# Making the low part of every fourth weight tile with a second ScalarE pass and an adding transfer instead of a VectorE subtraction

## The chip, the cores and the metric

One core of a Trainium2 chip runs one decoder layer on 256 tokens. The metric is the device time of one execution in microseconds (us). The engines are TensorE (PE: matmuls; PEld: its weight loads), VectorE (DVE), ScalarE (ACT), GpSimd (POOL) and SyncE (SP, which here only issues transfers). Sixteen DMA engines move the data.

## The reference

One layer on x of shape (1, 256, 1024), in float32. Cut to what matters:

```
h    = rms_norm(x, ln1_g)
q, k, v, z, xbc, dt, gate_a, gate_b = split(h @ w_in)           # w_in: 1024 x 10272
y_a  = moba_attention(norm(q), norm(k), v) @ w_o_attn
y_b  = mamba2_mixer(z, xbc, dt, ...) @ w_o_ssm
x    = x + (sigmoid(gate_a) * y_a + sigmoid(gate_b) * y_b) @ w_out
x    = x + (silu(h2 @ w_gate) * (h2 @ w_up)) @ w_down           # h2 = rms_norm(x, ln2_g)
x    = x + (p @ w_ple_proj) * sigmoid(h3 @ w_ple_gate)          # h3 = rms_norm(x, ln3_g)
```

Nearly all the work is matrix products of 256 token rows with some 100 MB of float32 weights, each of which is read from memory once.

## The kernel before

**Three products for one.** A float32 operand is cut into two parts of a faster matmul type (fp32r): a high part, which is the operand rounded, and a low part, which is the operand less the high part. A product is then a_high·w_high + a_high·w_low + a_low·w_high, three matmuls into one accumulator (`Panel.step`; `rows_step` for the panels that are computed with the weights as the stationary operand).

**Weight tiles.** The weights come in tiles of 128 partitions x 2 x 512 values, 512 KB each (`w_tiles`). A tile has three buffers: `raw`, as it is loaded (four buffers in turn), `wh`, the high part (four), and `wl`, the low part (five). For each tile, `load_tiles` issues the load on SP (L346) and calls `split_w`, where ScalarE writes wh from raw (the helper `act`, L213) and VectorE writes wl = raw - wh (L334). TensorE reads wh first and wl straight after it, 12 to 24 matmuls to a tile. A buffer is written again when its last reader is done: wh of tile n+4 when TensorE is done with tile n, wl of tile n+5 likewise, raw of tile n+4 when the split of tile n is done. The first eight tiles go another way (`load_first`); from there on every tile goes through `load_tiles`, and this document counts tiles from there, from 0 to 179.

**What sets the order.** TensorE's products over the weights follow one another in the order of the table `PANELS` (and after it w_o_attn, w_out, the gate and up weights, w_down, w_ple_gate); each is pinned behind the one before it (`queue`, `follow`). Between them stand background products: the transposes and convolution inputs, the attention scores and values, and the state-space scan. Generators (`Filler`) hand these out by due times that are written out by hand (`LAG`). All other engines get their order from the framework's scheduler: it goes through a timeline of its own and takes what is ready there by priority. The weight split has the first rank ("w"), then the emptying of accumulators ("ev"), then the background ("bg"). So a change to one helper can move instructions on every engine. Each engine runs its instructions strictly in the order that it was given, and one that waits holds up all that stand behind it.

**GpSimd's part.** It has few instructions between 50 and 310 us: 16 mask-like selections for the scan (`decay_rows`, L726, written to the four buffers `rr`, each of which must first be released by TensorE), eight inverse square roots of eight columns for the q and k norms (L662), and the four pairs that make `r_ssm` for the group norm (L462, L463).

Of the kernel before, what the change touches and what calls it, by code (L numbers as in the profile page):

```python
# [13 lines left out]
ALU = mybir.AluOpType  # L14
# [43 lines left out]
    ('yb', 3, None),  # L58
]
NFF = 11  # L60

NORMED = 5
BY_ROWS = [kind in ('xbc', 'z') and n >= NORMED for n, (kind, _, _) in enumerate(PANELS)]
# [91 lines left out]
def tile_layer(ctx: ExitStack, tc: tile.TileContext, head, xk, pt, vec, w_dt, w_big, w_dn2, w_pp, out):  # L155
    nc = tc.nc
# [3 lines left out]
    @contextmanager  # L160
    def prio(c):
        saved = tc.cur_priority
        tc.cur_priority = counters[c]
        yield
        counters[c] = tc.cur_priority
        tc.cur_priority = saved
# [45 lines left out]
    def act(o, i, f=AF.Copy, **kw):  # L212
        return nc.scalar.activation(o, i, f, **kw)  # L213
# [12 lines left out]
    def follow(ins, before):  # L226
        tc.add_manual_dep(
            ins, before.name, mybir.DependencyInfo(mybir.DependencyClass.NoSync, mybir.DependencyReason.DATA),
            reason="order of the tensor engine")
# [85 lines left out]
        load_head(xraw[k // 2][:, k % 2 : k % 2 + n])  # L315

    chunk_no = [0]

    def w_tiles():
        return (sb.tile([P, 2, 512], F32, tag="raw", bufs=4, name=nm("raw")),  # L320
                sb.tile([P, 2, 512], F32R, tag="wh", bufs=4, name=nm("wh")),
                sb.tile([P, 2, 512], F32R, tag="wl", bufs=5, name=nm("wl")))

    def split_w(tiles, js=slice(0, 2), c=WHOLE, on=None):

        raw, wh, wl = (t[:, js, c] for t in tiles)
        if on is None:
            rounded = act(wh, raw)
        elif on == c:
            rounded = nc.vector.tensor_copy(wh, raw)  # L330
        else:
            rounded = act(tiles[1][:, js, HALVES[0]], tiles[0][:, js, HALVES[0]])
            nc.vector.tensor_copy(tiles[1][:, js, on], tiles[0][:, js, on])
        nc.vector.tensor_sub(wl, raw, wh.bitcast(F32))  # L334
        return rounded
# [4 lines left out]
    def load_tiles(src, nk, behind=None):  # L340


        with prio("w"):
            for k in range(0, nk, 2):
                tiles = w_tiles()
                nc.sync.dma_start(tiles[0], src[:, k : k + 2])  # L346
                rounded = split_w(tiles)
                if behind is not None and behind[k // 2] is not None:
                    follow(rounded.ins, behind[k // 2])
                yield tiles  # L350

    def load(src, nk):

        return [part for tiles in load_tiles(src, nk) for part in parts_of(tiles)]
# [40 lines left out]
    def next_src():  # L395
        c = w_big[chunk_no[0]]
        chunk_no[0] += 1
        return c
# [657 lines left out]
    for n, (kind, i, _) in enumerate(PANELS):  # L1056
# [5 lines left out]
        if BY_ROWS[n]:  # L1062
            to = s4([4, T])
            for jj in range(2):
                tiles = load_tiles(next_src(), 4)
                wide = (kind, i) in WIDE
                if wide:
                    u = s2([2, T])
                else:
                    ps = psg.tile([P, 2, T], F32, tag="g", name=nm("g"))  # L1070
                for j, w in enumerate(tiles):
                    if wide:
                        ps = psg.tile([P, 512], F32, tag="g", name=nm("g"))
                    for k in range(8):
                        rows_step(ps if wide else ps[:, j], w, k, h_n, wide)
                    if wide:
                        with prio("ev"):
                            act(u[:, j], ps[:, T:])
                            nc.vector.tensor_add(u[:, j], ps[:, :T], u[:, j])  # L1079
                evac_rows(kind, i, jj, u if wide else ps, to)  # L1080
            fill.spawn(end_rows(kind, i, to), 0)
            continue
# [165 lines left out]
    h2 = res2.acts[0] + res2.acts[1]  # L1248
    for n in range(2 * NFF):

        tiles = load_tiles(next_src(), 4, [(None, res2.scaled), (fill.rounded, fill.rounded)][n] if n < 2 else None)
        pss = [psg.tile([P, 512], F32, tag="g", name=nm("g")) for _ in range(2)]
        if n == 0:

            tiles = list(tiles)
            for k in range(8):
                for ps, w in zip(pss, tiles):
                    rows_step(ps, w, k, h2, True)
        else:
            for ps, w in zip(pss, tiles):  # L1260
                for k in range(8):
                    rows_step(ps, w, k, h2, True)
        gate_up(n, *pss)
# [24 lines left out]
def _layout(i):  # L1288
# [5 lines left out]
    def kt(w):  # L1294

        return w.reshape(-1, P, w.shape[1]).transpose(1, 0, 2)

    def chunks(w, c0, k0, nk):
        return kt(w[k0 * P : (k0 + nk) * P, c0 : c0 + 512])
# [20 lines left out]

    gu = kt(gu).reshape(P, 8, 2, 2 * NFF, P).transpose(3, 0, 2, 1, 4).reshape(2 * NFF, P, 4, 512)
    big += [chunks(f["w_out"], 512 * n, 4 * g, 4) for g in range(2) for n in range(2)]
# [39 lines left out]
```

## Time and profile before

| | |
|---|---|
| time, median of 3 runs | 587.11 us (586.98 to 587.22) |
| span of the profiled execution, first to last instruction | 586.0 us |
| around the span (median less span) | 1.1 us |
| PE / DVE / ACT / POOL busy | 580.7 / 454.3 / 347.8 / 48.8 us |
| L334, wl = raw - wh, on VectorE | 193 instructions, 230.8 us |
| L213, wh from raw, on ScalarE | 192 instructions, 199.4 us |
| moved by DMA | 104.98 MB |

The page gives no time of the profiled execution but its span; the median of the runs stands for it. Busy time is the time in which an engine executes, without its waits. In a group's row stand the line, the engine, the operation, what it writes and reads by the program's names, the count, then busy time in us and the mean of one in ns, then the idle time of the engine just ahead of these instructions, with what ended most of it. In a row of the timeline stand the start in us, the duration in us, and in brackets the idle time ahead of it with what released it. A line number can be that of a helper: every ScalarE activation has L213 and nearly every matmul L232.

### The profile page before, as it was taken

Reading aid. Unit: us, or ns where it says so; the run is one execution under the profiler, and the core shown is the slowest. Engines: PE = TensorE matmul, PEld = TensorE weight load, DVE = VectorE, ACT = ScalarE, POOL = GpSimd, SP = SyncE. Lnnn points to the kernel's source line nnn. Section 1 sums busy time; section 2 is a strip of 40 time slices with the busy share of each in tenths; the row PEclk is TensorE's granted clock in tenths of the full one; section 3 lists DMA queues with packets and bytes.
Section 4 is the critical chain, followed back from the end, with each engine's and each line's share of the span. In section 5 each row is a group of like instructions: output and inputs, shape, how many; then the busy total and the mean of one; then the engine's idle time right before and its main releaser. Section 6 shows DMA issues by size and latency. Waiting matters only on the chain.

```text
span 586.0 us, 8990 instructions
## 1 busy us (share of the span) xinstructions
PE 580.7 (99%) x3245; PEld 493.6 (84%) x3245; DVE 454.3 (78%) x763; ACT 347.8 (59%) x598; POOL 48.8 (8%) x62
## 2 busy tenths in 40 slices
PE   9999999999999999999999999999999999999996
PEld 8887888988988888888887888888888888888885
DVE  6668899998889999998856765787777777546464
ACT  7846675775757569566654345775555555435452
POOL 2021120000412502000000000000000000000010
PEclk9999999999999999999999999999999999999999
DMA  9875545454553653554554675375556555665531
GB/s 325 312 233 181 180 152 181 144 181 148 160 161 102 204 186 112 193 150 141 155 186 145 200 261 175 105 248 190 184 185 189 188 192 181 192 196 188 181 107 72
DMA packets 33419, 104.98 MB, mean 179 GB/s; under 512 B 3712, under 2 KB 7136, under 8 KB 33376
## 3 DMA queue, kind: packets, MB, share of 16 engines
q1 hardware_dynamic: 33088, 104.03, 55.1%
q8 instruction: 25, 0.41, 0.3%
q10 hardware_dynamic: 288, 0.39, 0.2%
q14 instruction: 18, 0.15, 0.1%
HBM read 103.28 MB, written 1.06 MB: 178 GB/s over the span
## 4 chain that ended last, share of the span: by engine, by line
PE 99%; DVE 0%; ACT 0%; issue 0%
PE g L232 89%; PE pb L232 6%; PE pb L254 3%; PE pb L266 1%; ACT s L213 0%; DVE s L1281 0%; DVE s L1282 0%
## 5 line engine op out<-in xcount | busy, mean ns | idle before, releaser
L334 DVE TENSOR_TENSOR wl<-raw,wh 128x1024 fp32r<-128x1024 f32 (+2 forms) x193 | 230.8, 1199 | 102.4 <-ACT wh L213 101.7
L213 ACT ACTIVATE wh<-raw 128x1024 fp32r<-128x1024 f32 (+2 forms) x192 | 199.4, 1041 | 176.7 <-PE g L232 94.5
L232 PE MATMUL g<-wh,s 128*128 128x512 f32 (+1 forms) x836 | 262.3, 391 | 0.0
L232 PE MATMUL g<-s,wh 128*128 128x512 f32 (+1 forms) x736 | 236.1, 380 | 0.0
L232 PEld LDWEIGHTS g<-wh,s 128*128 128x128 f32 x836 | 156.9, 189 | 32.0 <-issue 0.5
L232 PE MATMUL g<-s,wl 128*128 128x256 f32 x672 | 177.2, 281 | 0.0
L232 PE MATMUL g<-wl,s 128*128 128x512 f32 (+1 forms) x418 | 161.1, 388 | 0.0
L232 PEld LDWEIGHTS g<-s,wh 128*128 128x128 f32 x736 | 129.9, 189 | 21.0 <-DVE s L1111 0.2
L232 PEld LDWEIGHTS g<-s,wl 128*128 128x128 f32 x672 | 127.0, 189 | 7.1
L232 PEld LDWEIGHTS g<-wl,s 128*128 128x128 f32 x418 | 78.5, 188 | 15.7 <-DVE wl L334 0.4
L213 ACT ACTIVATE s<-s 128x256 fp32r<-128x256 f32 (+4 forms) x75 | 41.4, 555 | 13.7 <-DVE s L1166 5.0
L213 ACT ACTIVATE s<-g 128x256 f32<-128x256 f32 (+1 forms) x94 | 38.4, 411 | 5.9 <-PE g L232 3.3
L213 ACT ACTIVATE s<-pb 128x512 f32<-128x512 f32 (+3 forms) x53 | 24.5, 484 | 15.7 <-PE pb L254 7.9
L596 DVE SCALAR_TENSOR_TENSOR s<-s,vecs,s 128x255 f32<-128x255 f32 (+2 forms) x72 | 33.6, 489 | 0.0
L232 PE MATMUL pb<-s,s 128*64 128x128 f32 (+5 forms) x336 | 29.3, 294 | 0.0
L232 PEld LDWEIGHTS pb<-s,s 128*64 128x64 f32 (+2 forms) x336 | 24.0, 158 | 6.2 <-issue 3.2
L726 POOL TENSOR_SCALAR_AFFINE_SELECT rr<-a_h 128x512 fp32r<-128x512 f32 x16 | 17.0, 1079 | 121.5 <-PE pb L232 104.7
L254 PE MATMUL pb<-ident,s 128*128 128x128 f32 x170 | 25.7, 273 | 0.0
L254 PEld LDWEIGHTS pb<-ident,s 128*128 128x128 f32 x170 | 20.5, 140 | 3.8 <-issue 0.3
L1175 POOL TENSOR_TENSOR tiny<-ss 128x1 f32<-128x1 f32 x4 | 1.4, 340 | 266.8 <-ACT s L213 266.8
L213 ACT ACTIVATE s<-s,vecs 128x256 f32<-128x256 f32 (+1 forms) x40 | 20.3, 557 | 3.2 <-DVE s L1079 3.1
L662 POOL TENSOR_TENSOR tiny<-tiny,mhalf 128x8 f32<-128x8 f32 x8 | 15.3, 1913 | 42.2 <-DVE tiny L660 38.3
(138 smaller groups left out, 328.6 us busy)
## 6 DMA issues: line engine op xcount, KB each, us to landing
raw<-in_w_big SPq DMA_DIRECT2D x176, 512.0 KB
raw<-in_head SPq DMA_DIRECT2D x4, 512.0 KB
s<-in_xk SPq DMA_DIRECT2D x4, 512.0 KB
raw<-in_head SPq DMA_DIRECT2D x6, 256.0 KB
s<-e_d SPq DMA_DIRECT2D x8, 128.0 KB
raw<-in_w_pp SPq DMA_DIRECT2D x2, 512.0 KB
raw<-in_w_dn SPq DMA_DIRECT2D x2, 512.0 KB
out<-s SPq DMA_DIRECT2D x3, 256.0 KB
```

Source lines behind the costliest of these rows:

```text
L213: return nc.scalar.activation(o, i, f, **kw)
L232: ins = nc.tensor.matmul(o, lhsT, rhs, start=start, stop=stop).ins
L254: queue(nc.tensor.transpose(o, i, ident[: i.shape[0], : i.shape[0]]).ins, main)
L266: nc.tensor.matmul(pw[:, :P], zero, zero, start=True, stop=True)
L334: nc.vector.tensor_sub(wl, raw, wh.bitcast(F32))
L596: stt(cc[j][:, sft:], pu[:, j, : T - sft], cw[j][3 - sft], cc[j][:, sft:], op0=ALU.mult, op1=ALU.add)
L662: nc.gpsimd.tensor_tensor(f, ms, mhalf, op=ALU.pow)
L726: nc.gpsimd.affine_select(r, bcast(a_h[:, c, h0 : h0 + 4].bitcast(F32), P), pattern=[[0, 4], [1, P]], compare_op=ALU.is_ge, fill=0.0, base ...
L1175: nc.gpsimd.tensor_add(sss, self.ss[:, tt, 0:1], self.ss[:, tt, 1:2])
```

## The change

For 18 of the tiles, numbers 16, 20, 24 and so on to 84, VectorE's subtraction is left out. ScalarE makes a second pass over raw and writes the rounded tile with the sign turned into wl, and GpSimd then issues a transfer that reads the same 512 KB of the weights from memory once more and adds them to wl. The other tiles are made as before.

```diff
+BY_DMA = range(16, 88, 4)
...
+    tile_no = [-1]
...
                 tiles = w_tiles()
                 nc.sync.dma_start(tiles[0], src[:, k : k + 2])
-                rounded = split_w(tiles)
+                tile_no[0] += 1
+                if tile_no[0] in BY_DMA:
+                    rounded = act(tiles[1], tiles[0])
+                    act(tiles[2], tiles[0], scale=-1.0)
+                    nc.gpsimd.dma_start(tiles[2], src[:, k : k + 2], accum_op=ALU.add)
+                else:
+                    rounded = split_w(tiles)
```

The scheduler then gives every engine a somewhat other order. In what follows, line numbers are nine higher after the change, and the numbers in the names of buffers are not the same in both.

On ScalarE, around tile 64: its buffers are wh_2758 before, and wl_2771 and wh_2770 after. The rows with `s_486` are the exponentials of one step of the attention, `g_2534` and `g_2545` are an accumulator that is being emptied. Before:

```order
L213 ACTIVATE wh_2729<-raw_2728 128x1024
L213 ACTIVATE s_473_2497<-g_2534 128x256
L213 ACTIVATE s_503_2632<-pb_2630 128x512
L213 ACTIVATE s_486_2539,tiny_2538<-s_486_2539,tiny_2537 128x128
L213 ACTIVATE s_486_2539,tiny_2538<-s_486_2539,tiny_2537 128x256
L213 ACTIVATE s_486_2539,tiny_2538<-s_486_2539,tiny_2537 128x128
L213 ACTIVATE wh_2758<-raw_2757 128x1024
L213 ACTIVATE s_486_2539,tiny_2538<-s_486_2539,tiny_2537 128x256
```

and after:

```order
L215 ACTIVATE s_452_2402<-s_473_2508,vecs 128x256
L215 ACTIVATE s_503_2644<-pb_2642 128x512
L215 ACTIVATE s_486_2550,tiny_2549<-s_486_2550,tiny_2548 128x128
L215 ACTIVATE s_486_2550,tiny_2549<-s_486_2550,tiny_2548 128x256
L215 ACTIVATE s_486_2550,tiny_2549<-s_486_2550,tiny_2548 128x128
L215 ACTIVATE s_486_2550,tiny_2549<-s_486_2550,tiny_2548 128x256
L215 ACTIVATE wl_2771<-raw_2769 128x1024
L215 ACTIVATE wh_2770<-raw_2769 128x1024
```

The new pass stands ahead of the tile's own wh, and both behind the last of the exponentials. So it is, with a few other rows between at some tiles, at all 18 tiles: wl ahead of wh.

On GpSimd, at the same place. Before:

```order
L726 AFFINE_SELECT rr_2958<-a_h 128x512
L726 AFFINE_SELECT rr_2962<-a_h 128x512
L462 TENSOR_SCALAR tiny_2646<-tiny_2641 128x2
L463 TENSOR_TENSOR r_ssm<-tiny_2646,mhalf 128x2
L462 TENSOR_SCALAR tiny_3030<-tiny_3025 128x2
```

and after:

```order
L735 AFFINE_SELECT rr_2971<-a_h 128x512
L735 AFFINE_SELECT rr_2975<-a_h 128x512
L354 DMA wl_2771<-in_w_big 128x1024
L471 TENSOR_SCALAR tiny_2658<-tiny_2653 128x2
L472 TENSOR_TENSOR r_ssm<-tiny_2658,mhalf 128x2
L354 DMA wl_2993<-in_w_big 128x1024
L354 DMA wl_3102<-in_w_big 128x1024
L354 DMA wl_3221<-in_w_big 128x1024
```

The 18 new transfers stand between the selections, the norms' inverse roots and the r_ssm pairs: whatever waits there holds up a transfer behind it, and a transfer that waits for ScalarE holds them up.

On TensorE, at one step of the attention scores (rows that write `pb`) in the products of tiles 20 and 21 (`g_1026` before, `g_971` and `g_1028` after). Before:

```order
L232 MATMUL g_1026<-s_77_452,wl_1022 128x256
L232 MATMUL pb_987<-s_65_429,s_100_560 128x128
L232 MATMUL pb_986<-s_65_429,s_100_560 128x128
L232 MATMUL g_1026<-s_79_458,wh_1021 128x512
L232 MATMUL g_1026<-s_79_458,wl_1022 128x256
```

and after:

```order
L234 MATMUL g_971<-s_81_464,wl_966 128x256
L234 MATMUL pb_989<-s_65_429,s_100_560 128x128
L234 MATMUL pb_988<-s_65_429,s_100_560 128x128
L234 MATMUL g_971<-s_81_464,wh_965 128x512
L234 MATMUL g_971<-s_81_464,wl_966 128x256
```

The first two score products have moved ahead by some ten rows, into the tile before. The weight products keep their order; background products move among them. Runs of background products that stand between weight products number 74 before and 79 after, with the same products in them.

## The prediction

> **What bounds the kernel now.** I read the page first: the engines' shares, the chain that ended last, and the groups that the change touches.
>
> ```profile
> span 586.0 us, 8990 instructions
> PE 580.7 (99%) x3245; PEld 493.6 (84%) x3245; DVE 454.3 (78%) x763; ACT 347.8 (59%) x598; POOL 48.8 (8%) x62
> ...
> PE 99%; DVE 0%; ACT 0%; issue 0%
> ...
> L334 DVE TENSOR_TENSOR wl<-raw,wh 128x1024 fp32r<-128x1024 f32 (+2 forms) x193 | 230.8, 1199 | 102.4 <-ACT wh L213 101.7
> L213 ACT ACTIVATE wh<-raw 128x1024 fp32r<-128x1024 f32 (+2 forms) x192 | 199.4, 1041 | 176.7 <-PE g L232 94.5
> ```
>
> The chain that ended last is TensorE for 99% of the span. A busy TensorE need not be a full one, so I asked the waits of its weight loads for the low part; the columns are us in total, times, longest.
>
> ```profile
> PEld pb L232 <- DVE wl L334: 0.5, 2, 0.4
> PEld g L232 <- DVE wl L334: 0.4, 1, 0.4
> ```
>
> TensorE's loads waited 0.9 us for VectorE's wl in the whole program. Last the stretch in which the changed tiles are used, 72 to 308 us, whole and for wh alone (columns: length, then busy time and count of PE, PEld, DVE, ACT and in the first row POOL, granted clock, DMA share, GB/s).
>
> ```profile
> 72.00:308.00 236.00, 236.00 (x1492) 202.41 (x1492) 215.57 (x409) 155.82 (x299) 33.34 (x28) 1.00 0.50 159
> 72.00:308.00 236.00, 186.60 (x612) 109.12 (x611) 83.65 (x69) 71.94 (x68) 1.00 0.50 159
> ```
>
> VectorE is busy for 215.57 of 236 us there (91%), ScalarE for 155.82 (66%), the DMA engines for half of it; TensorE for all of it, at full clock. VectorE is nearly full and yet hardly anyone waits for it, because the split runs ahead of TensorE. So the change relieves an engine that isn't on the path. It can win only the little that TensorE loses to waits; it can lose whatever TensorE has to wait for a late wl.
>
> **What it removes.** 18 subtractions of 1.20 us (L334), 21.6 us of VectorE; its share in the stretch falls to 194 of 236 us. On the path this is worth at most the 0.9 us of waits above, and those lie over the whole program; I put it at nothing.
>
> **What it adds on ScalarE.** 18 passes of 1.04 us (the wh row), 18.7 us; its share rises to 174.5 of 236 us (74%). A quarter stays idle, and the cover is the lead of wh over TensorE, which the next rows show; if it were gone, a ScalarE pass would cost 1.04 us each. Behind the new pass stand wh of the same tile and accumulators to be emptied, each 1 us later at worst; I put it at nothing too.
>
> **What it adds in front of TensorE: the chain to wl.** Before, wl came 1.2 us behind wh. Now: ScalarE's negated pass, then GpSimd's issue, then the transfer, then TensorE. How long may that take? Since the new pass stands directly or closely ahead of the tile's wh, I count from where wh began before to TensorE's first use of wl. Of the 18 tiles the tightest is tile 28, the widest tile 36; tile 64 is the one whose order is shown above (ScalarE starts wh; TensorE's first matmul on wl).
>
> ```profile
> 103.60 1.05 ACT L213 ACTIVATE wh<-raw 128x1024 fp32r<-128x1024 f32 x1
> 111.18 0.28 PE L232 MATMUL g<-s,wl 128*128 128x256 f32 x1
> ...
> 128.17 1.07 ACT L213 ACTIVATE wh<-raw 128x1024 fp32r<-128x1024 f32 x1 [0.35 <-ACT s L213]
> 142.51 0.29 PE L232 MATMUL g<-s,wl 128*128 128x256 f32 x1
> ...
> 227.85 1.06 ACT L213 ACTIVATE wh<-raw 128x1024 fp32r<-128x1024 f32 x1
> 236.71 0.39 PE L232 MATMUL g<-wl,s 128*128 128x512 f32 x1
> ```
>
> That is 7.6, 14.3 and 8.9 us; the median of the 18 is 9.7. If the new pass ends where wh began, these are what is left for GpSimd and the transfer. If it only starts there, because ScalarE had no room earlier, 1.06 us less: 6.5 for the tightest, 8.6 for the median. And if ScalarE has room, it is more, since the five wl buffers let the pass start when TensorE leaves the tile five before: four tiles of 236/68 = 3.47 us ahead of the use, 13.9 less 1.06 makes 12.8 us.
>
> How long do GpSimd and the transfer take? No transfer is issued by GpSimd in this trace and none adds, so I bound it. GpSimd's part by its own two groups, the transfer by the load queue and by a 256 KB load that ScalarE waited for, with its issue, the two loads ahead of it and the end of the wait:
>
> ```profile
> L726 POOL TENSOR_SCALAR_AFFINE_SELECT rr<-a_h 128x512 fp32r<-128x512 f32 x16 | 17.0, 1079 | 121.5 <-PE pb L232 104.7
> L662 POOL TENSOR_TENSOR tiny<-tiny,mhalf 128x8 f32<-128x8 f32 x8 | 15.3, 1913 | 42.2 <-DVE tiny L660 38.3
> ...
> q1 hardware_dynamic: 33088, 104.03, 55.1%
> ...
> 287.45 1.50 SPq L346 DMA_DIRECT2D raw<-in_w_big  x2
> 289.00 0.42 SPq L1128 DMA_DIRECT2D s<-in_pt  x1
> ...
> 295.15 0.63 ACT L213 ACTIVATE s<-s 128x512 fp32r<-128x512 f32 x1 [1.23 <-DMA s<-in_pt]
> ```
>
> GpSimd: 1.1 to 1.9 us. The queue moved 104.03 MB in 55.1% of 586 us, so 512 KB (0.524 MB) take 0.551 x 586 x 0.524 / 104.03 = 1.63 us of all sixteen engines. The 256 KB load took 295.15 - 289.00 = 6.15 us; less its own 0.8 and the two loads ahead of it, 3.3, a fixed 2.1 us is left (an estimate). An adding transfer must read what it adds to as well: between once and twice 1.63 us. Beside it run the raw loads, half of the engines' time: none to two of them ahead. Bounds: 1.1 + 2.1 + 1.6 = 4.8 us, and 1.9 + 2.1 + 3.3 + 3.3 = 10.6 us. I take 1.1 + 2.1 + 2.4 + 0.8 = 6.4 us, GpSimd by the selection (its other operation is a power, further from issuing), the adding halfway, half a load ahead.
>
> [...]
>
> With 6.4 us the chain is inside even the tightest case (6.5): TensorE doesn't wait, and the price is 0. With 7 us the later reading gives 0.5 us over all 18 tiles, with 8 us 2.9, with 9 us 10.9, with 10.6 us some 33; by the earlier reading 0, 0.4, 2.6 and some 18 (each sum adds up, over the 18 tiles, by how much the chain is longer than what is left).
>
> **What it moves.** Raw buffers of the 18 tiles come free after two ScalarE passes instead of wh and the subtraction, about as late. The transfers add 18 x 0.524 = 9.4 MB, 9%, to engines that are half idle; 0. On GpSimd r_ssm, the selections and the roots stand behind transfers that wait for ScalarE; at tile 64 r_ssm would follow the new pass, and r_ssm is wanted only when the following group is emptied, a tile or two later: 0, and if a root came late by one tile, about 3.5 us once.
>
> TensorE's background products move. A break in the weight products costs time of its own; this is the step shown above, before:
>
> ```profile
> 89.07 0.40 PE L232 MATMUL g<-s,wh 128*128 128x512 f32 x1
> 89.31 0.28 PE L232 MATMUL g<-s,wl 128*128 128x256 f32 x1
> 89.52 0.33 PE L232 MATMUL pb<-s,s 64*128 64x128 f32 x2
> 89.77 0.51 PE L232 MATMUL g<-s,wh 128*128 128x512 f32 x1
> 90.12 0.28 PE L232 MATMUL g<-s,wl 128*128 128x256 f32 x1
> 90.23 0.39 PE L232 MATMUL g<-s,wh 128*128 128x512 f32 x1
> ...
> 91.86 0.85 PE L232 MATMUL pb<-s,s 64*128 64x128 f32 x10
> 92.63 0.73 PE L232 MATMUL g<-s,wh 128*128 128x512 f32 x2
> ```
>
> From start to start, a pair wl, wh takes 0.11 + 0.24 us where nothing stands between (90.12 to 90.23, 89.07 to 89.31), and a score product 0.077 (ten from 91.86 to 92.63). With two of these between, wl to the next wl takes 90.12 - 89.31 = 0.81 instead of 0.35 + 0.15: a break costs 0.3 us. There are 79 instead of 74 breaks, +1.5 us if all five new ones are of this kind. Most breaks are by transposes, which cost far less, and some score groups come to stand beside transposes, with no break of their own: down to -0.7 us when I price each pair of neighbours at what it took before. I take -0.3.
>
> **Sum.** 0 (VectorE) + 0 (ScalarE) + 0.1 (a tile that may miss by a little) + 0 (queues) - 0.3 (order) = -0.2 us against the profiled execution: span 585.8. The median is 1.1 us above the span, so 586.9 us.
>
> **The rivals.** About 0.2%, 1.17 us, is what a measurement of this kernel can tell from no change: 585.94 to 588.28 us counts as the same.
>
> *The low part comes too late.* The mechanism: the chain through GpSimd takes 8.5 to 9.5 us instead of 6.4, and at the tiles with the least left TensorE stands at its first load of wl, which nothing makes up, since TensorE is the bound. It decides from about 7.5 us on. For it speaks that two of its parts are unseen, and that GpSimd is erratic where VectorE is full: the same selection took
>
> ```profile
> 145.01 0.64 POOL L726 TENSOR_SCALAR_AFFINE_SELECT rr<-a_h 128x512 fp32r<-128x512 f32 x1 [62.65 <-PE pb L232]
> 183.09 3.28 POOL L726 TENSOR_SCALAR_AFFINE_SELECT rr<-a_h 128x512 fp32r<-128x512 f32 x1 [14.37 <-PE pb L232]
> ```
>
> 0.64 us and 3.28 us, and 2.6 us more make 9.0 of my 6.4. Against it: the ring of five wl buffers allows 12.8 us on average. Price at 9 us: 2.6 to 10.9, the middle 6.8, so 593.7 us. Chance 0.33. [...]
>
> *GpSimd's queue becomes the bound of the background.* A root or an r_ssm pair behind a waiting transfer is late, an accumulator stays full, TensorE stops. Price: one tile, 3.5 us, once or twice, 590 to 594. Against it: GpSimd is busy for 33.3 of the 236 us. Chance 0.05.
>
> *Faster.* The order wins its 0.7, the waits go, and a little more with them: 585.6 us or less. For it: nothing beyond these 1.6 us, since TensorE has no other waits. Chance 0.08.
>
> That the transfers don't do what they say I give no chance: the order shows 18 of them, each waiting for ScalarE.
>
> **How the numbers follow.** Forecast 0.54, late wl 0.33, queue 0.05, faster 0.08. The likeliest case gives 586.9. Its own range is 586.0 to 588.2. The range reaches down to 585.8, through most of the faster case, and up to 595, past the middle of the late case, which leaves its upper end out, about 1 in 8. Faster 0.08, same 0.54, slower 0.38.
>
> **What would show it.** In the profile after: on ScalarE 18 rows wl from raw of 1.04 us; VectorE with 175 subtractions; the chain still 99% TensorE; weight loads of wl waiting for a DMA less than 1 us in total; from the end of a negated pass to the first matmul on that wl more than the transfer needs, which I expect at 6.4 us. I am wrong if TensorE's waits name a DMA into wl with more than 1 us, if a GpSimd issue takes over 2 us, or if TensorE has fewer than 99% of the chain.

## The result and the profile after

| | before | after |
|---|---|---|
| median of the runs taken together | 587.16 us (586.98 to 587.68, 4 runs) | 591.12 us (589.68 to 592.50, 4 runs) |
| ratio, 95% interval | | 1.0064 (1.0050 to 1.0079) |
| span of the profiled execution | 586.0 us | 590.8 us (its time 592.50) |

The change makes the kernel slower by 0.64%, 4 us; forecast was 586.9 us, no difference. One thing about the times first: later runs list a span beside each time, and there 1.7 to 2.0 us lie around the span in every execution, 1.7 to 1.8 in those of the kernel before (585.3 us of span for 587.07 us, 586.3 for 588.08). So the profiled execution of before, with 586.0, was one of some 587.7 us, and the 1.1 us of the table above was a median set against another execution's span. The forecast is a difference and isn't touched by it.

The page after: busy times, two transfer queues (packets, MB, share of the engines), the chain, and the groups that the change touches.

```profile
span 590.8 us, 9020 instructions
PE 583.5 (99%) x3245; PEld 493.7 (84%) x3245; DVE 434.5 (74%) x745; ACT 364.1 (62%) x616; POOL 59.9 (10%) x80
...
q1 hardware_dynamic: 33088, 104.03, 52.2%
q0 software_dynamic: 2592, 9.44, 9.1%
...
PE 96%; DMA 3%; ACT 0%; DVE 0%; issue 0%
...
L337 DVE TENSOR_TENSOR wl<-raw,wh 128x1024 fp32r<-128x1024 f32 (+2 forms) x175 | 208.5, 1193 | 103.6 <-ACT wh L215 102.9
...
L354 POOL DMA_DIRECT2D wl<-in_w_big x18 | 16.2, 898 | 135.6 <-ACT wl L215 60.1
...
wl<-in_w_big POOLq DMA_DIRECT2D x18, 512.0 KB, 8.3
```

VectorE lost 18 subtractions, ScalarE got 18 passes, as said. New are q0, the queue of GpSimd's transfers, with 9.1% of sixteen engines' span, and the last row: 8.3 us (median) from GpSimd's issue to the landing, where the whole chain was put at 6.4. The chain that ended last, all TensorE before, now holds 3% of DMA. The waits of TensorE's loads and matmuls name it (total, times, longest):

```profile
PEld g L234 <- DMA wl<-in_w_big: 3.6, 4, 2.3
PE g L234 <- DMA wl<-in_w_big: 1.8, 1, 1.8
```

Of the 3.6 us that weight loads waited, part lay beside running matmuls; the second row, 1.8 us, is what TensorE itself stood. The chain in order of time (start, length, what) gives the places, tile 80 and tile 84:

```profile
286.97 0.27 issue
287.23 9.56 DMA wl<-in_w_big
296.80 0.04 issue
296.84 4.14 PE g L234 x17
300.99 0.95 ACT wl L215
301.94 0.29 issue
302.23 8.93 DMA wl<-in_w_big
311.16 0.04 issue
311.20 5.77 PE g L234 x17
```

Followed backwards, TensorE at 311.20 waited for a transfer issued at 302.23, and that for a negated pass. Why was the pass no earlier? ScalarE's timeline says it, with the idle time in brackets:

```profile
293.75 0.19 ACT L215 ACTIVATION_READ_ACCUMULATOR s<-s,tiny 128x1 f32 x1
298.45 0.63 ACT L215 ACTIVATE s<-s 128x512 fp32r<-128x512 f32 x1 [4.52 <-DMA s<-in_pt]
298.99 2.00 ACT L215 ACTIVATE wh<-raw 128x1024 fp32r<-128x1024 f32 x2
300.89 1.04 ACT L215 ACTIVATE wl<-raw 128x1024 fp32r<-128x1024 f32 x1
```

ScalarE waited 4.52 us for the load of p where before it waited 1.23: the transfer of tile 80 ran from 287.23 to 296.8, beside that load. Last, five microseconds from the end of the stall, with the granted clock (third number from the end):

```profile
311.25:316.25 5.00, 5.00 (x15) 3.96 (x16) 1.98 (x2) 1.54 (x2) 0.00 (x0) 0.66 0.65 242
```

The clock was 0.66 on average: 5 x 0.34 = 1.7 us lost once more (an estimate from these two numbers). So the 4.8 us by which the span grew are: 2.0 at tile 84 (its first matmul on wl started 2.2 us after the matmul ahead of it, where 0.23 is usual), 1.7 of clock behind it, 0.24 at tile 80, and some 0.9 in smaller pieces; the kernel without transfers, below, shows where the larger of them lie.

### The profile page after: what moved, and what is told of

It reads as the page before. It is cut to its first block, busy times and chain, and to the rows that moved or that the text cites. A ratio compares the mean times of both kernels' runs of the same rounds, so it can differ in the third digit from the quotient of the medians.

```text
span 590.8 us, 9020 instructions
## 1 busy us (share of the span) xinstructions
PE 583.5 (99%) x3245; PEld 493.7 (84%) x3245; DVE 434.5 (74%) x745; ACT 364.1 (62%) x616; POOL 59.9 (10%) x80
## 4 chain that ended last, share of the span: by engine, by line
PE 96%; DMA 3%; ACT 0%; DVE 0%; issue 0%
PE g L234 87%; PE pb L234 6%; DMA wl<-in_w_big 3%; PE pb L256 3%; PE pb L268 1%; ACT wl L215 0%; ACT s L215 0%; DVE s L1290 0%; DVE s L1291 0%
## 5 line engine op out<-in xcount | busy, mean ns | idle before, releaser
L337 DVE TENSOR_TENSOR wl<-raw,wh 128x1024 fp32r<-128x1024 f32 (+2 forms) x175 | 208.5, 1193 | 103.6 <-ACT wh L215 102.9
L354 POOL DMA_DIRECT2D wl<-in_w_big x18 | 16.2, 898 | 135.6 <-ACT wl L215 60.1
L735 POOL TENSOR_SCALAR_AFFINE_SELECT rr<-a_h 128x512 fp32r<-128x512 f32 x16 | 15.3, 967 | 54.5 <-PE pb L234 43.1
```

The lines of the kernel that those rows point to most:

```text
L354: nc.gpsimd.dma_start(tiles[2], src[:, k : k + 2], accum_op=ALU.add)
L735: nc.gpsimd.affine_select(r, bcast(a_h[:, c, h0 : h0 + 4].bitcast(F32), P), pattern=[[0, 4], [1, P]], compare_op=ALU.is_ge, fill=0.0, base ...
```

## The experiments

Each is the changed kernel with the edit shown (some are set against another kernel told of here, and say so), timed in five rounds beside the kernel before.

**First: is it tile 84?** I began with theory A as "TensorE stands at tile 84, because the p load makes its pass late". Its rivals: the new order (B), a fixed cost around the span (C), a chain that is too long by itself (A2). Four kernels.

```diff
-BY_DMA = range(16, 88, 4)
+BY_DMA = range(16, 84, 4)
```

> Tile 84 goes back to VectorE's subtraction; the other 17 keep pass and transfer, and TensorE's order is that of the changed kernel. Theory A (the loss is TensorE standing 2 us at tile 84, whose transfer starts late because ScalarE waited for the p load, and a granted clock of 0.83 for some 10 us behind that stall in part of the executions): no wait of more than 0.5 us for a DMA into wl, clock 1.00 all the way, 587.0 to 588.0 us. Rival B (the new order of TensorE's background products and the ScalarE passes cost time everywhere): 589 us or more. Rival C (0.6 us around the span, for the use of GpSimd's transfers at all) adds to A: time less span 1.7 us, 587.6 to 588.0.

590.28 us (589.30 to 592.47), 1.0047 (1.0034 to 1.0061). A as it stood is wrong: without tile 84 nearly all of the loss stays. In its profile TensorE stands elsewhere; this is tile 16, which lost a quarter of a microsecond in the profile of the changed kernel, though up to tile 84 the two kernels have the same instructions in the same order:

```profile
72.29 0.63 PE L234 MATMUL g<-s,wh 128*128 128x512 f32 x2
73.85 0.38 PE L234 MATMUL g<-s,wl 128*128 128x256 f32 x1 [0.93 <-DMA wl<-in_w_big]
```

C falls too: 1.7 us around the span, as in the kernel before.

```diff
-BY_DMA = range(16, 88, 4)
+BY_DMA = (84,)
```

> Only tile 84 gets the pass and the transfer, the other 17 keep VectorE's subtraction; TensorE's order is that of the kernel before. Theory A with its cause (the p load lands 3 us late because the transfer of tile 80 runs beside it): with no transfer at tile 80 the p load takes 6 to 7 us again, the negated pass comes 2 to 3 us earlier, and TensorE waits 0 to 0.6 us; 587.0 to 588.0 us. Rival A2 (at tile 84 the chain is too long by itself, whatever ran before): a wait of 1.5 us or more, 589 to 592 us. Rival C: time less span 1.7 us here too.

587.70 us (587.32 to 591.31), 1.0007 (0.9995 to 1.0019): nothing lost in the middle of the runs, though two of eleven took 589.03 and 591.31. With no transfer at tile 80 the p load cost ScalarE 1.43 us instead of 4.52, and the negated pass began at 297.86 instead of 300.89:

```profile
295.42 0.63 ACT L215 ACTIVATE s<-s 128x512 fp32r<-128x512 f32 x1 [1.43 <-DMA s<-in_pt]
```

TensorE waited for no transfer. So that cause is right for tile 84, and A2 wrong there.

```diff
         p_l = s2([2, T], F32R)
-        act(p_h, praw)
-        nc.vector.tensor_sub(p_l, praw, p_h.bitcast(F32))
...
+    with prio("w"):
+        follow(act(p_h, praw).ins, last_wh[0])
+        nc.vector.tensor_sub(p_l, praw, p_h.bitcast(F32))
```

Here last_wh[0] is the newest wh pass in program order, eight tiles on.

> All 18 tiles as in the changed kernel, TensorE's order too; ScalarE's pass that rounds p stands behind the passes of eight more tiles, so that the queue no longer waits for the p load. Theory A with its cause: the negated pass of tile 84 starts 2 us or more earlier (298.9 us or before instead of 300.9), the wait at tile 84 falls from 2.0 to at most 0.5 us, no clock drop behind it, 587.3 to 588.3 us. Rival A2: the wait stays at 1.5 us or more, 589 to 592.5. Rival B: 589 to 592.5.

590.35 us (589.19 to 591.00), 1.0044 (1.0032 to 1.0056). At tile 84 the pass began at 299.81, 1.1 us earlier and not the 2 that A wanted, and TensorE didn't wait. But TensorE came to that tile 1.9 us later than in the changed kernel, so this run doesn't tell what the earlier pass alone is worth. For in this execution it stood at tile 16 once more, and shortly at 64 and 40:

```profile
72.55 0.63 PE L234 MATMUL g<-s,wh 128*128 128x512 f32 x2
74.92 0.39 PE L234 MATMUL g<-s,wl 128*128 128x256 f32 x1 [1.75 <-DMA wl<-in_w_big]
```

```diff
                     act(tiles[2], tiles[0], scale=-1.0)
-                    nc.gpsimd.dma_start(tiles[2], src[:, k : k + 2], accum_op=ALU.add)
```

> All 18 negated passes and the changed kernel's order on TensorE, ScalarE and VectorE, without the 18 transfers: the raw tile is not added, so wl is only the rounded tile with the sign turned. Theories A and C: 586.4 to 587.3 us, time less span 1.1 us, and the granted clock 1.00. Rival B: 589 us or more. By the working of the forecast the order alone gives -0.3 us, 586.8.

587.54 us (587.33 to 588.24), 1.0002 (0.9993 to 1.0011). The 18 ScalarE passes and the whole new order cost nothing, and VectorE's relief brings nothing: B falls, and all of the loss comes with the transfers. That also bounds the change from below: transfers that took no time at all would only bring back the time before.

This kernel and the changed one have the same instructions in the same order on every engine but for the transfers. So TensorE's lag behind it can be followed from tile to tile, in one execution of each (start of the first matmul on the tile's wl, us):

| tile | 15 | 18 | 63 | 66 | 79 | 82 | 86 |
|---|---|---|---|---|---|---|---|
| changed kernel | 70.37 | 80.83 | 234.29 | 243.96 | 292.52 | 303.07 | 320.09 |
| without the transfers | 69.81 | 80.02 | 233.49 | 242.85 | 291.41 | 301.60 | 314.85 |
| lag | 0.56 | 0.81 | 0.80 | 1.11 | 1.11 | 1.47 | 5.24 |

The 0.56 stood there before the first transfer was wanted. The lag grows by 0.25 at tile 16, 0.3 at 64, 0.4 at 80, and 3.8 at 84 with the clock drop behind it. Over the other fourteen transfers (20 to 60, and 68 to 76) it doesn't grow at all. In this execution nothing was lost but where wl came late.

So theory A became wider: the chain from negated pass to wl takes 8 to 9 us. That is as long as the room (from the end of the negated pass to TensorE's first matmul on wl) at some six tiles, and at which of them it bites changes from execution to execution (the changed kernel itself took 589.7 us twice and 592.5 twice). The trace's packet records (a transfer of 512 KB is 128 packets of 4 KB here), taken tile by tile, fit: in the profile of the changed kernel the last packet landed 6.1 to 9.4 us behind the pass's end (median 8.25), and TensorE wanted wl 7.0 to 15.0 us behind it (median 10.7). At tiles 16, 64, 80 and 84 TensorE began 0.5 us after the last packet, at 52 and 40 0.9 and 1.0: those have half a microsecond to spare at most. Its rivals now: GpSimd's way of issuing (D), and traffic or ScalarE's time, whoever waits (E).

**Second: shorten the chain, lengthen it, let nobody wait.**

```diff
-                    nc.gpsimd.dma_start(tiles[2], src[:, k : k + 2], accum_op=ALU.add)
+                    nc.gpsimd.dma_start(tiles[2], src[:, k : k + 2])
```

> The 18 transfers on GpSimd's queue only copy: raw is written over the negated tile instead of being added, so wl is the whole weight. Every engine's order is that of the changed kernel. Theory A (TensorE waits because the chain from negated pass to wl takes 8 to 9.5 us, more than is left at some tiles, and half of the transfer's own time is the adding): a packet falls from 328 ns to the 160 to 170 of the raw loads, the chain by 1.3 us to about 7, the waits for a DMA into wl to at most 0.6 us in all; 587.5 to 588.5 us. Rival D (what is long is GpSimd's way of issuing, whatever the transfer does): the chain stays at 8 us or more, the waits at 2 us or more, 589 to 592.5 us.

587.92 us (587.40 to 588.48), 1.0004 (0.9996 to 1.0013), and no wait of TensorE for a transfer. The same queue, issuer, bytes and order, only no adding, and the loss is gone. Its rows:

```profile
q0 software_dynamic: 2592, 9.44, 5.5%
...
L354 POOL DMA_DIRECT2D wl<-in_w_big x18 | 10.4, 575 | 135.3 <-ACT wl L215 66.8
...
wl<-in_w_big POOLq DMA_DIRECT2D x18, 512.0 KB, 6.8
```

Set against the rows of after: one transfer takes 9.1% x 590.8 / 18 = 2.99 us of all sixteen engines when it adds, 5.5% x 586.3 / 18 = 1.79 when it copies; issue to landing 8.3 against 6.8; GpSimd's issue 0.90 against 0.58. D as stated falls.

```diff
-                    act(tiles[2], tiles[0], scale=-1.0)
+                    follow(act(tiles[2], tiles[0], scale=-1.0).ins, rounded.ins)
```

> The same 18 tiles, but the negated pass stands behind the pass for wh of the same tile, so every chain starts about 1.1 us later. Theory A: the tiles with less than 1 us to spare in the changed kernel (16, 40, 52, 64, 80, 84) each lose 0.6 to 1.1 us more, 4 to 6 us together, with clock drops behind the longer stalls: 593 to 598 us. Rival E (the loss comes from the traffic or from ScalarE's time, not from when wl is there): no further loss, 589.5 to 592.5 us.

626.51 us (621.13 to 627.55), 1.0644 (1.0615 to 1.0673): in A's direction, far beyond its size. The pass of tile 16, ahead of which nothing had stalled, began at 65.73 instead of 63.47, 2.3 us later and not 1.1, since ScalarE's other work also went ahead of it; at most of the later tiles, with the stalls taken off, the room shrank by 1 to 5 us. TensorE's matmuls stood at eleven tiles:

```profile
PEld g L234 <- DMA wl<-in_w_big: 29.9, 11, 5.6
PE g L234 <- DMA wl<-in_w_big: 25.5, 11, 5.2
```

25.5 us of standing and a mean clock of 0.979 over 624.5 us, some 13 us, come close to the 38.5 us that the span grew (624.5 against 586.0), though a drop that falls into a stall is counted twice in that sum.

```diff
-                    act(tiles[2], tiles[0], scale=-1.0)
-                    nc.gpsimd.dma_start(tiles[2], src[:, k : k + 2], accum_op=ALU.add)
+                    act(tiles[2][:, 1], tiles[0][:, 1], scale=-1.0)
+                    nc.vector.tensor_sub(tiles[2][:, 0], tiles[0][:, 0], tiles[1][:, 0].bitcast(F32))
+                    nc.gpsimd.dma_start(tiles[2][:, 1], src[:, k + 1], accum_op=ALU.add)
```

> Of the 18 tiles only the second half is negated by ScalarE and added to by a transfer, of 256 KB; VectorE subtracts the first half. Theory A: the transfer has half the packets (1.3 us of the engines' time less) and its half is wanted some 1.7 us later, so TensorE waits at most 0.3 us in all: 587.2 to 588.3 us. Rival D: the chain hardly shortens, 588.5 to 590 us.

589.52 us (589.02 to 591.45), 1.0042 (1.0029 to 1.0055): a miss for A's number. The chain did shorten (6.7 us from issue to landing), and at 17 tiles TensorE had some 2.2 us or more to spare. At the other, tile 28, the scheduler had put the pass behind a step of the attention's exponentials:

```profile
105.51 0.19 ACT L215 ACTIVATION_READ_ACCUMULATOR s<-s,tiny 128x1 f32 x1
105.60 0.62 ACT L215 ACTIVATE wl<-raw 128x512 fp32r<-128x512 f32 x1
```

It ran at 105.60, where the changed kernel ran it at 101.63, and TensorE stood there:

```profile
112.15 0.40 PE L234 MATMUL g<-s,wh 128*128 128x256 f32 x2
113.43 0.38 PE L234 MATMUL g<-s,wl 128*128 128x256 f32 x1 [0.88 <-DMA wl<-in_w_big]
```

That is 0.9 us in this execution, whose span is 587.3; the last kernel below shows what this one place is worth. (Its expectation gives the stall as 2.0 us: there I had added a weight load's wait to the matmul's, and they are the same stall.)

```diff
+    spare = const.tile([P, 2, 512], F32R, name="spare")
...
-                    act(tiles[2], tiles[0], scale=-1.0)
-                    nc.gpsimd.dma_start(tiles[2], src[:, k : k + 2], accum_op=ALU.add)
+                    act(spare, tiles[0], scale=-1.0)
+                    nc.vector.tensor_sub(tiles[2], tiles[0], tiles[1].bitcast(F32))
+                    nc.gpsimd.dma_start(spare, src[:, k : k + 2], accum_op=ALU.add)
```

> All 18 negated passes and all 18 adding transfers are made, at the same tiles, but into a spare buffer that nobody reads; wl is made by VectorE's subtraction as before. Theory A: nobody waits for a transfer, so nothing is lost: 587.2 to 588.3 us. Rival E (traffic, ScalarE's passes or the use of GpSimd's queue cost time by themselves): 589 us or more. The chain can be measured in it with VectorE as full as before: 8 to 9.5 us.

599.70 us (596.17 to 602.00), 1.0202 (1.0178 to 1.0225), and useless as a control: with no wl buffer to wait for, the spare pass moved ahead of the arrival of its raw tile, and ScalarE stood.

```profile
ACT spare L215 <- DMA raw<-in_w_big: 35.1, 16, 8.1
```

**Third: a better control, and the tiles sorted by room.** The first edit is set against the kernel just told of.

```diff
-                    act(spare, tiles[0], scale=-1.0)
+                    follow(act(spare, tiles[0], scale=-1.0).ins, rounded.ins)
```

> As the kernel whose transfers nobody waits for, mended: there ScalarE's pass into the spare buffer had come to stand ahead of the arrival of its raw tile, and ScalarE waited 35 us for raw loads; here each spare pass stands behind the pass for wh of its tile. All 18 passes and all 18 adding transfers are made, and wl comes from VectorE's subtraction. Theory A: nobody waits for a transfer, so little is lost: 587.2 to 588.4 us, ScalarE's wait for raw loads under 6 us as in the kernel before. Rival E (the traffic of the adding transfers or ScalarE's passes cost by themselves): 589.5 us or more with ScalarE not waiting for raw loads.

589.69 us (589.13 to 590.68), 1.0043 (1.0029 to 1.0057): above A's range and in E's, though nobody waits for a transfer. ScalarE still waits 6.1 us for raw loads (1.5 in the kernel before), and TensorE's weight loads wait for ScalarE, among others by these rows; the changed kernel has the first two not at all, and the third with 0.3:

```profile
PEld pb L234 <- ACT wh L215: 1.1, 3, 0.4
PEld pb L234 <- ACT s L215: 1.1, 3, 0.5
PEld g L234 <- ACT s L215: 0.8, 2, 0.5
```

So 18 more passes on ScalarE need not be free in every order, as they are in the change's own (the kernel without transfers). This kernel lost 2.2 us; its order differs from that of both others and VectorE keeps all its subtractions, so how much of it is ScalarE's, the order's or the traffic's stays open. E is not cleared by this control; for the change's own order the table above clears it, and the copying transfers and the last kernel below speak against it too.

```diff
-BY_DMA = range(16, 88, 4)
+BY_DMA = (20, 24, 32, 36, 48, 56, 60, 68, 72, 76)
```

> Only the ten tiles with more than 10 us from the negated pass to the use of wl in the changed kernel (20, 24, 32, 36, 48, 56, 60, 68, 72, 76) are made by transfer. Theory A: the chain of 8 to 9.4 us fits everywhere, no wait of more than 0.4 us for a DMA into wl, 587.2 to 588.3 us. Rival E (each transfer costs about the same, 3 us for 18): 589.0 to 589.7 us.

588.60 us (587.47 to 592.69), 1.0022 (1.0007 to 1.0037): between the two. In the profile TensorE stood once, 0.7 us at tile 56, where GpSimd was busy when the pass was done:

```profile
196.35 3.69 POOL L671 TENSOR_TENSOR tiny<-tiny,mhalf 128x8 f32<-128x8 f32 x1 [4.63 <-DVE tiny L669]
199.99 0.92 POOL L354 DMA_DIRECT2D wl<-in_w_big  x1
```

The pass had ended at 197.89; an inverse root of 3.69 us stood ahead, and the chain took 11.2 us. The rival of the forecast about GpSimd's queue is real, once.

```diff
-BY_DMA = range(16, 88, 4)
+BY_DMA = (16, 28, 40, 52, 64, 80, 84)
```

> The seven tiles with less than 10 us from the negated pass to the use of wl in the changed kernel (16, 28, 40, 52, 64, 80, 84) are made by transfer, the others not. Theory A: nearly the whole loss stays, 589.0 to 592 us, with waits for a DMA into wl at two or more of them. Rival E (each transfer costs about the same): 588.5 to 589.0 us.

593.65 us (592.26 to 595.20), 1.0106 (1.0087 to 1.0124): seven transfers cost 6 us, more than all eighteen and above A's upper end; ten others cost 1.1. The price of a transfer is set by its place, and E, with the same price for each, falls. TensorE stood at tiles 28 and 84 (here tile 28's pass began at 104.49 instead of 101.63), and a little at 16:

```profile
113.25 0.38 PE L234 MATMUL g<-s,wl 128*128 128x256 f32 x1 [1.02 <-DMA wl<-in_w_big]
312.04 0.50 PE L234 MATMUL g<-wl,s 128*128 128x512 f32 x1 [1.52 <-DMA wl<-in_w_big]
```

**Last: half transfers without the one late pass.** Beside this line, the edit is that of the half transfers above.

```diff
-BY_DMA = range(16, 88, 4)
+BY_DMA = [t for t in range(16, 88, 4) if t != 28]
```

> As the kernel that adds to the second half of the tile alone, without tile 28, the one tile where TensorE waited for a transfer in it (2.0 us: its negated pass had come to stand behind a step of the attention's exponentials and ran 4 us later). 17 tiles, 256 KB each. Theory A (what is lost is lost where the low part is late, and nowhere else): no wait for a DMA into wl above 0.3 us, 587.1 to 588.2 us, the time of the kernel before, although VectorE is relieved of 17 half subtractions. Rival E (each transfer costs something wherever it lies): the loss stays at 1.5 us or more, 589 to 589.5 us.

587.63 us (587.15 to 589.97), 1.0000 (0.9987 to 1.0013), and TensorE waits for no transfer. (The kernel before ranged from 587.07 to 589.89 beside it.) Seventeen adding transfers of 256 KB, each with some 2.5 us or more to spare, cost nothing, and win nothing. No version beat the kernel before, and by this road there is next to nothing to win: the kernel without transfers has shown that a relieved VectorE is worth nothing here.

## Why the prediction was wrong, point by point

- **What bounds the kernel**: right. TensorE is the bound, and VectorE's relief is worth 0: 21.6 us less of VectorE with all passes made, 1.0002 (0.9993 to 1.0011).
- **ScalarE put at nothing**: right for this order, by the same kernel; the mended control leaves open whether in every order.
- **The order, -0.3 us**: within what can be measured (-0.1). Breaks by transposes do cost less: in the profile before, the wh product behind six of them led the next product by 0.32 us (301.64 to 301.96) where 0.23 is usual, so such a break cost 0.1 us against the 0.3 of one by two score products.
- **"Queues: 0"**: wrong in one thing that the part on what moves left out. It counted the 9.4 MB as 9% of half-idle engines and didn't ask which load the transfers run beside. The p load came 3.3 us later (ScalarE took it up at 298.45 instead of 295.15), that pass stands in ScalarE's queue, and the next negated pass stands behind it.
- **The chain, 6.4 us**: this is the step that failed. Forecast were 3.2 us for GpSimd and the fixed part, 2.4 for the transfer's own moving ("the adding halfway") and 0.8 for loads beside it ("half a load ahead"). Measured, as means over the 18: 0.4 us from the pass's end to GpSimd's issue, 2.6 from there to the first packet (1.6 at the least), 5.1 from the first packet to the last, and 0.5 from the last packet to TensorE where it had been waiting; together 8.6. In the 5.1 the sixteen engines gave 3.0 us to the transfer and 2.0 to raw loads. So the fixed part was 0.3 us too short, the adding 0.6, and the loads beside it 1.2: each term was too small, and that for the loads by the most. The transfer of tile 84 shows the sharing, in the stretch in which its packets moved (queue: packets, MB, share of 16 engines):

```profile
q0 software_dynamic: 143, 0.52, 49.5%
q1 hardware_dynamic: 322, 1.16, 43.2%
```

That is from 303.9 to 310.7 us: 49.5% of 6.8 us, 3.4, for the transfer, and as much again, 2.9, for 1.16 MB, more than two raw loads. The engines stood "half idle" on average; but in the stretches in which the 18 transfers moved they were idle for 0.2 us of 5.1. An average share was read where a stretch had to be.

- **The adding, put halfway between one copy and two**: it took 2.99 us of the engines against 1.79 for the copy on the same queue, 1.67 times, and against the 1.63 of a raw load before, 1.83 times. How much of that is the reading of wl no trace shows.
- **"GpSimd's erratic times" as the reason for the late rival**: not the main one. GpSimd issued 0.29 us after the pass at most tiles, and its issue took 0.90 us. What varied is the time from its issue to the first packet, 1.57 to 4.26 us. A full VectorE doesn't go with the long ones: at tile 24 VectorE was busy all through and the first packet came after 1.57 us; at tile 76 it was idle for over a third of the time and it came after 3.19. Wherever it took over 3 us, 118 or more packets of raw loads lay between; but at tiles 24, 32 and 68, with 100 to 123 of them, it took only 1.6 to 1.7, so what makes it long stays open.
- **The rival that came true**: the late low part, 0.33, deciding "from about 7.5 us on". The chain to TensorE took 8.6 us. Summed over the 18 tiles as in the forecast, that makes 1.2 us by the earlier reading of what is left and 7.0 by the later (2.6 and 10.9 at the 9 us that the rival priced); measured are 4.0, of which standing for wl is only a part. Its middle, 593.7, was too high. The earlier reading is the nearer: tile 28 had 8.8 us from the pass's end, where 7.6 or 6.5 were counted. Two of the three signs of being wrong came true as well: 3.6 us of loads waiting for a DMA into wl, and 96% of the chain on TensorE.
- **What the sum did not have**: the clock behind a stall, some 1.7 us in the profiled execution. The execution of 592.45 us shows none (a mean clock of 1.000); where it lost its time is not on record.

## What to carry to other kernels

When work goes from an engine to a transfer, the engine's busy share is not what is at stake: compare the transfer's whole latency (here 8.6 us on average), in the very stretch where it runs and with the loads that run there, with the room that its reader leaves at the tightest tile (here 7.0). Where the bound engine hardly waits, as here (0.9 us for wl in the whole program), such a move can't win and can lose at a handful of places, and these differ from execution to execution; a profile of one execution names only some of them. Ask too which other loads the new traffic delays, and who stands in an in-order queue behind them.

## What the runs showed of the hardware

An adding transfer of 512 KB from memory took 2.99 us of all sixteen engines, a copying one on the same queue 1.79; GpSimd needed 0.90 us to issue the one and 0.58 for the other.

In the profile before, seven products in plain float32 at the start (128 columns, two instructions each) took from 0.83 to 4.12 us, 0.47 each; the eight in fp32r right behind them, of 256 columns, took from 4.12 to 6.07, 0.24 each.

TensorE's clock fell behind some of its stalls and not behind others. Here are the five microseconds behind four stalls of the kernel whose passes come later, in which TensorE had been idle for 2.63, 2.04, 1.44 and 4.41 us (the clock is the third number from the end):

```profile
76.00:81.00 5.00, 5.00 (x26) 4.60 (x27) 4.10 (x10) 0.60 (x1) 1.38 (x2) 0.71 0.45 162
163.90:168.90 5.00, 4.97 (x21) 4.34 (x22) 2.52 (x5) 0.91 (x3) 0.00 (x0) 0.66 0.54 173
179.80:184.80 5.00, 4.99 (x49) 4.30 (x50) 3.34 (x7) 0.63 (x1) 0.00 (x0) 1.00 0.67 221
211.25:216.25 5.00, 4.99 (x15) 3.93 (x16) 0.09 (x1) 0.50 (x1) 0.00 (x0) 0.66 0.47 177
```

Over all the profiles here, the nine stalls of 1.82 us or more (the shortest is tile 84 of the changed kernel) each came with a drop, and the twelve others of over half a microsecond, up to 1.75 us (tile 16 of the kernel with the later p pass), none; one that fell into a drop already running is left out. Five microseconds at 0.66 are 1.7 us lost, so the stall of 1.82 us cost some 3.5 (an estimate from these numbers).

In the clock records of the traces each of these drops is a clock of 0.50 for 3.41 us (1.7 us lost, as by the windows), and for 6.83 us at two of the longest stalls (5.16 us here, 4.15 in the first kernel with a spare buffer). In the kernel of the later passes they begin at 75.47, 164.22, 212.00, 259.79, 293.92 and 345.12 us, whole multiples of 3.41 us apart.
